# Distances between the addresses of streamed tiles and weights, one for each feed-forward stage of a decoder trunk, and the last stage streamed from its last column to its first

## The chip, the cores and the metric

The kernel runs on one core of a Trainium2 chip. The metric is the device time of one execution in microseconds (us). Before the change it is 1928.77 us, the median of two runs (1928.66 and 1928.88).

## The reference

Two decoder layers on 512 tokens of width 1024 in float32. Each layer is a feed-forward half-step, an attention and another feed-forward half-step; the first layer's attention is stick-breaking, the second's a sliding window with sinks.

```python
def swiglu(h, w_gate_up, w_down):
    gate, up = jnp.split(h @ w_gate_up, 2, axis=-1)
    return (jax.nn.silu(gate) * up) @ w_down
...
    for i in range(DEPTH):
        x = x + 0.5 * swiglu(rms_norm(x, norm_gains[i, 0]), ffn_w_gate_up[i, 0], ffn_w_down[i, 0])
        h = rms_norm(x, norm_gains[i, 1])
        ...
        x = x + 0.5 * swiglu(rms_norm(x, norm_gains[i, 2]), ffn_w_gate_up[i, 1], ffn_w_down[i, 1])
```

The inner width is 2816. The change concerns the four feed-forward stages, called 0 to 3 here; the stages run in the order 0, stick-breaking attention, 1, 2, sliding-window attention, 3.

## The kernel before

All activations are kept transposed: features on the 128 partitions, the 512 tokens as columns. A product of the width-1024 input is a sum over 8 blocks of 128 features, and every float32 operand is split into a high and a low float32r part, so that each term takes three matmuls: high weights by high input, high weights by low input, low weights by high input (`terms`). In each matmul a 128x128 block of weights is loaded into the array and a tile of 512 columns is streamed past it; the sum goes to a PSUM bank.

In a feed-forward stage (`ffn`), gate and up take 2 x 22 output tiles of 24 matmuls each, 1056 in all. Streamed are `xh0` to `xh7` and `xl0` to `xl7` (128 x 512 float32, 2048 bytes a partition), the weights lie in `whi` and `wlo`. The results leave PSUM through the vector engine and the scalar engine (`swiglu`), which write `hh0` to `hh21` and `hl0` to `hl21`. The down product has 8 output tiles of 66 matmuls, 528 in all; it streams the `hh` and `hl` tiles. The profile calls the two kinds of matmul `gu` and `dn` by their PSUM tiles.

Weights come as a stream of units (`queue`), each of 1024 or 896 columns, through rings of three buffers: a DMA writes `raw`, the scalar engine casts it to `whi` (L181), the vector engine (or GpSimd in the attentions) subtracts to get `wlo` (L186, L184). When the matmuls of a unit are done (`release`), the next unit is opened, cast and its successor's DMA issued. TensorE runs strictly in program order; all its matmuls are recorded by one helper and have line L75 in the profile, so they are told apart by their tiles. While one matmul streams its columns, the weights of the next are loaded.

The attentions' projections use the same ring. The input projections stream `xh` and `xl` (or stream weights past them), the output projections (PSUM tile `op`) stream the attention's `oh` and `ol`. At the start of the output projection of the sliding-window attention, weights are also put in spare tiles called `qw`.

Where tiles lie matters for this change. A pool places tiles one behind the other along the partition, in the order of their first use: constants, then the weight rings and the `xh`/`xl` tiles (pool `work`), then the pool of the stage. A block of weights is 512 bytes a partition, a streamed tile 2048, so within one stage all blocks of one weight tile, and all streamed tiles, have the same address modulo 128. In the program before, in bytes modulo 128: `whi` and `wlo` 96, `xh`/`xl` 96, `hh`/`hl` 64, the stick-breaking `oh`/`ol` 64, the window's `oh`/`ol` 96, `qw` 0. The distance, streamed address minus weight address, is then 0 in gate/up, 96 in down, 96 in the stick-breaking output projection, 0 in the window's, and 96 in the latter where the weights are in `qw`. (Modulo 512 the window's is 256, the others as said.)

Of the kernel before, what the change touches and what calls it, by code (L numbers as in the profile page):

```python
# [7 lines left out]
F32 = mybir.dt.float32  # L8
F32R = mybir.dt.float32r
# [6 lines left out]
P = 128  # L16
T = 512
TB = T // P
D = 1024
KD = D // P  # L20
# [4 lines left out]
HD = 64  # L25
PAIRS = HEADS // 2
CHUNKS = HEADS // 4
EPS = 1e-6
UNITS = 3
WARM = 40  # L30
POOL_SQUARES = 6
# [7 lines left out]
NROT = ROT // 2  # L39
# 500000 ** (-arange(0, 16, 2) / 16) in float32  # L40
INV_FREQ = [
# [23 lines left out]
class _Ordered:  # L65
    """an engine whose instructions stay in the order of the program"""

# [19 lines left out]
class _Filler:  # L87
    """tensor-engine work that fills the waits of an attention step: a generator that yields its cost,
    or None when nothing is ready"""

# [17 lines left out]
class _Trunk:  # L108
    def __init__(self, tc, pools, psum, aps):
        self.tc, self.nc = tc, _Engines(tc)  # L110
        self.const, self.work = pools
        self.psum = psum
        self.aps = aps
        self.units = []
        self.raw, self.ready = [], []
        self.taken = self.spent = 0
        self.roped = False
        self.extra = -1

# [1 line left out]
    def mm(self, out, lhs, rhs, start, stop):  # L121
        self.nc.tensor.matmul(out, lhs, rhs, start=start, stop=stop)

# [3 lines left out]
    def terms(self, out, pairs, first=True, last=True, release=()):  # L127
        """out = sum of w * x over pairs ((w_hi, w_lo), (x_hi, x_lo)): three float32r passes each;
        release: the terms that are the last of a unit of the weight stream, or 1: the last"""
        n = len(pairs)  # L130
        cost = 3 * max(out.shape[-1], 256) / 2400.0
        for i, ((wh, wl), (xh, xl)) in enumerate(pairs):
            self.mm(out, wh, xh, start=(first and i == 0), stop=False)
            self.mm(out, wh, xl, start=False, stop=False)
            self.mm(out, wl, xh, start=False, stop=(last and i == n - 1))
            if i in ((n - 1,) if release == 1 else release):
                self.release(1)
            yield cost
# [7 lines left out]

# [1 line left out]
    def queue(self, ap, pool=False):  # L148
        self.units.append((ap, ap.shape[1], pool))

    def _load(self, pieces=1):
# [8 lines left out]
    def _open(self, n):  # L160
        size = self.units[n][1]
        hi = self.work.tile([P, size], F32R, tag="whi", name=f"whi{n}", bufs=UNITS)
        lo = self.work.tile([P, size], F32R, tag="wlo", name=f"wlo{n}", bufs=UNITS)
        self.ready.append((hi, lo))

    def advance(self, hi, lo):
        """one more unit of the weight stream ahead, in tiles that the stage has free"""
        n = self.extra = len(self.ready)
        self.ready.append((hi, lo))
        self._part(n)  # L170
        self._load()
# [25 lines left out]
    def weights(self, a):  # L197
        """the next unit of the stream as [row, a, column] high and low parts"""
        hi, lo = self.ready[self.taken]
        self.taken += 1  # L200
        h3, l3 = (t.rearrange("p (a b) -> p a b", a=a) for t in (hi, lo))
        return [(h3[:, i, :], l3[:, i, :]) for i in range(a)]

# [1 line left out]
    def setup(self, which):  # L205
# [36 lines left out]

# [1 line left out]
    def norm_tile(self, k, which):  # L244
# [56 lines left out]

# [1 line left out]
    def swiglu(self, fp, f, gu):  # L303
# [12 lines left out]

    def ffn(self, following, first=False, rope=False):
        tc, nc = self.tc, self.nc
        with tc.tile_pool(name="ffn", bufs=1) as fp:
            hs, evac = [], []  # L320
            xs = list(zip(self.xh, self.xl))
            ahead = []
            if first:
                ahead = [(self.bank("gu"), self.weights(KD)) for _ in range(3)]
# [9 lines left out]
            for f in range(NF):  # L334
                gu = []
# [32 lines left out]

# [1 line left out]
    def stack(self, out, src):  # L370
        """a pair of heads (rows) to one [high | low] or [low | high] column of rows per head"""
        nc = self.nc
        for h in range(2):
            own, other = slice(h * HD, (h + 1) * HD), slice(HD - h * HD, 2 * HD - h * HD)
            nc.scalar.copy(out[own, h, :], src[own, :])
            nc.vector.tensor_sub(out[other, h, :], src[own, :], out[own, h, :])  # L376

    def project_pair(self, p, out, start=False):
        """q^T and k^T of a pair of heads, as exact high and low parts"""
        nc, ap = self.nc, self.ap  # L380
# [30 lines left out]
    def token_columns(self, evacuate, rows=None):  # L411
        """a chunk of 256 columns of an input projection, tokens on partitions"""
        w = self.weights(KD // 2) + self.weights(KD // 2)
        for b in range(TB):
            sl = slice(b * P, (b + 1) * P)
            ps = self.bank("tok")[:, : 4 * HD]
            yield from self.terms(ps, [((h[:, sl], l[:, sl]), w[k]) for k, (h, l) in enumerate(zip(self.xh, self.xl))], release=(KD // 2 - 1, KD - 1) if b == TB - 1 else ())
            if rows and b == 0:
                rows()
            evacuate(b, ps)  # L420

    def project_values(self, out):
        """v of four heads: [token, block, head, high | low]"""
        nc = self.nc
# [11 lines left out]
    def stick_scores(self, i, qk, out):  # L436
        """exclusive products of the kept lengths times beta, for one pair of heads and query block i"""
        nc, ap = self.nc, self.ap
# [25 lines left out]
    def stick_turn(self, i, beta, wt):  # L464
        """weights of query block i to keys on partitions, high and low parts"""
        nc = self.nc
# [47 lines left out]
    def fold(self, o, h, ps):  # L514
        """the products with the high and the low part of v are on rows of their own: add them"""
        t = self.ap.tile([HD, T], F32, tag="tmp", name="fold", bufs=2)
        self.nc.scalar.copy(t, ps[HD:, :])
        self.nc.vector.tensor_add(o[h * HD : (h + 1) * HD, :], ps[:HD, :], t)
# [8 lines left out]
    def project_early(self, parts, opened):  # L527
        """the first terms of the first output tiles, as far as parts are there"""
        self.settled, self.spare = len(parts), None
# [79 lines left out]

# [1 line left out]
    def rope_tables(self):  # L611
        """cos | cos and -sin | sin of every token's angles: [token, block, 16]"""
        self.roped = True
# [58 lines left out]

# [1 line left out]
    def rope(self, x, heads, engine):  # L674
        """x: [token, block, heads * HD], rotated in place"""
        nc, ap = self.nc, self.ap
# [11 lines left out]
    def head_factor(self, sq, heads, extra):  # L688
        """r * rsqrt(mean of squares of r * raw + eps) * extra, one per token, block, head"""
        nc, ap = self.nc, self.ap  # L690
# [57 lines left out]
    def window_queries(self, c, out):  # L748
        """four heads of q with head dims on partitions (two heads a tile), and their score factors"""
        nc, ap = self.nc, self.ap  # L750
# [20 lines left out]
    def window_scores(self, c, b, qt, y, out):  # L771
        """the softmax of four heads and one block of queries"""
        nc, ap = self.nc, self.ap
# [161 lines left out]

# [1 line left out]
    def store(self, n):  # L937
# [3 lines left out]
def build(tc, aps, stages="0s12w3"):  # L941
    from contextlib import ExitStack

    with ExitStack() as ctx:
# [4 lines left out]
        for st in stages:  # L949
            if st in "0123":  # L950
                i = int(st)
                for u in range(2 * NF):
                    net.queue(aps["gu"][i, u])
                for n in range(KD):
                    at = 0
                    for size in DOWN:
                        net.queue(aps["dn"][i, n, :, at * P : (at + size) * P])
                        at += size
# [18 lines left out]
        for i, st in enumerate(stages):  # L977
# [4 lines left out]
            if i == 0 and st in "0123":  # L982
                net.ffn(following, first=True)
                continue
            if stages[i + 1 : i + 2] == "w":
                net.ffn(following, rope=True)
                continue
            {"0": net.ffn, "1": net.ffn, "2": net.ffn, "3": net.ffn, "s": net.stick_breaking, "w": net.sliding_window}[st](following)

# [40 lines left out]
```

## Time and profile before

| what | value |
|---|---|
| median of two runs | 1928.77 us |
| span of the profiled execution | 1925.5 us |
| matmuls in it | 8994 |
| mean granted TensorE clock | 0.992 |
| gate/up of stages 0, 1, 2, 3 begins at | 32.7, 638.9, 1003.0, 1557.5 us |
| down of stages 0, 1, 2, 3 begins at | 250.3, 879.7, 1243.8, 1798.3 us |

The span runs from the first to the last instruction of the program; the time of a run has a few microseconds more around it. In the profile PE is TensorE's matmuls and PEld its weight loads, DVE the vector engine, ACT the scalar engine, POOL GpSimd, SP the engine that issues DMAs. [...] The chain of work that ended last is followed back from the last instruction, and its long pieces (start, duration, what, how many) give the time that so many matmuls took in a row.

### The profile page before, as it was taken

The page shows a single profiled execution, that of the slowest core. Times are in us where ns is not written, and L with a number is a line of the kernel's source. Part 1 is how long each engine was busy: PE and PEld are TensorE (multiplying, and loading weights), DVE is VectorE, ACT ScalarE, POOL GpSimd, SP SyncE. Part 2 cuts the span into 40 slices and gives each one's busy share as a digit, 9 for nine tenths or more (in the row PEclk, how much of TensorE's full clock was granted, in tenths as well). Part 3 has the DMA queues.
Part 4 walks back from the last instruction along what each step waited for, and adds up shares of the span by engine and source line. Part 5 has one row for each costly group of instructions (what it writes and reads, how often), then busy time and mean ns, then how long its engine had stood idle before and what let it go on. Part 6 is the DMA issues. An engine that isn't in the chain of part 4 may idle for free.

```text
span 1925.5 us, 22581 instructions
## 1 busy us (share of the span) xinstructions
PE 1895.7 (98%) x8994; PEld 1565.6 (81%) x8994; DVE 970.5 (50%) x1535; ACT 695.1 (36%) x1071; POOL 172.0 (9%) x131
## 2 busy tenths in 40 slices
PE   9999999999999999999999999999998999999999
PEld 7888888877887888888888888888887788888887
DVE  6444433378887644443235444423588664444321
ACT  5333222266675323332223333222357542223211
POOL 1000000233321000000000000000142210000000
PEclk9999999999999999999999999999989999999999
DMA  5233333321112333223333222333221122332331
GB/s 167 98 97 99 96 91 92 103 69 56 49 62 66 99 97 97 92 97 94 97 96 99 92 98 96 93 93 100 81 67 34 29 92 98 99 99 90 103 109 60
DMA packets 49930, 170.52 MB, mean 89 GB/s; under 512 B 5921, under 2 KB 6177, under 8 KB 49825
## 3 DMA queue, kind: packets, MB, share of 16 engines
q1 hardware_dynamic: 49824, 169.07, 27.9%
q8 instruction: 71, 1.16, 0.2%
q14 instruction: 35, 0.28, 0.0%
HBM read 166.96 MB, written 2.10 MB: 88 GB/s over the span
## 4 chain that ended last, share of the span: by engine, by line
PE 84%; DVE 8%; issue 4%; ACT 3%; POOL 1%; DMA 0%; SPq 0%; ACTq 0%; DVEq 0%; POOLq 0%
PE gu L75 49%; PE dn L75 23%; PE op L75 4%; PE tok L75 3%; DVE keep L459 2%; DVE beta L460 1%; PE pv L75 1%; DVE qs L376 1%; DVE wt L482 1%; ACT keep L453 1%; PE sc L75 1%; PE z L75 0%; PE ptr L75 0%; DVE e L793 0%; PE q L75 0%
## 5 line engine op out<-in xcount | busy, mean ns | idle before, releaser
L181 ACT CAST whi<-raw 128x1024 fp32r<-128x1024 f32 (+2 forms) x323 | 330.0, 1022 | 964.8 <-issue 361.6
L75 PE MATMUL gu<-xh,whi 128*128 128x512 f32 x1400 | 545.5, 390 | 1.4 <-ACT whi L181 1.4
L75 PE MATMUL gu<-xh,wlo 128*128 128x512 f32 x1400 | 545.0, 389 | 0.7 <-DVE wlo L186 0.7
L75 PE MATMUL gu<-xl,whi 128*128 128x512 f32 x1400 | 544.8, 389 | 0.5 <-DVE xl L253 0.5
L186 DVE TENSOR_TENSOR wlo<-raw,whi 128x1024 fp32r<-128x1024 f32 (+2 forms) x293 | 349.4, 1193 | 248.2 <-ACT whi L181 245.6
L75 PEld LDWEIGHTS gu<-xh,wlo 128*128 128x128 f32 x1400 | 262.8, 188 | 56.5 <-DVE wlo L186 1.8
L75 PEld LDWEIGHTS gu<-xh,whi 128*128 128x128 f32 x1400 | 262.9, 188 | 56.2 <-ACT whi L181 1.9
L75 PEld LDWEIGHTS gu<-xl,whi 128*128 128x128 f32 x1400 | 262.9, 188 | 55.3 <-DVE xl L253 0.9
L75 PE MATMUL dn<-hh,wlo 128*128 128x512 f32 x704 | 280.9, 399 | 0.0
L75 PE MATMUL dn<-hl,whi 128*128 128x512 f32 x704 | 277.4, 394 | 0.0
L75 PE MATMUL dn<-hh,whi 128*128 128x512 f32 x704 | 276.0, 392 | 0.0
L309 DVE TENSOR_TENSOR u<-gu,rbc 128x512 f32<-128x512 f32 x87 | 60.1, 691 | 274.7 <-PE gu L75 274.7
L75 PEld LDWEIGHTS dn<-hl,whi 128*128 128x128 f32 x704 | 132.1, 188 | 34.3
L75 PEld LDWEIGHTS dn<-hh,whi 128*128 128x128 f32 x704 | 132.2, 188 | 31.5
L75 PEld LDWEIGHTS dn<-hh,wlo 128*128 128x128 f32 x704 | 132.2, 188 | 30.5
L307 DVE TENSOR_TENSOR g<-gu,rbc 128x512 f32<-128x512 f32 x88 | 60.8, 691 | 176.5 <-PE gu L75 176.4
L261 POOL TENSOR_TENSOR acc<-acc,sq 128x512 f32<-128x512 f32 x30 | 46.4, 1547 | 1116.1 <-ACT sq L260 1116.1
L184 POOL TENSOR_TENSOR wlo<-raw,whi 128x512 fp32r<-128x512 f32 x60 | 87.5, 1483 | 164.9 <-ACT whi L181 164.9
L75 PE MATMUL tok<-whi,xh 128*128 128x256 f32 x288 | 86.4, 300 | 0.0
L75 PE MATMUL tok<-whi,xl 128*128 128x256 f32 x288 | 82.4, 286 | 0.1
L75 PE MATMUL tok<-wlo,xh 128*128 128x256 f32 x288 | 82.3, 286 | 0.1
L300 DVE SCALAR_TENSOR_TENSOR x<-dn,x 128x512 f32<-128x512 f32 x32 | 22.1, 691 | 116.5 <-PE dn L75 116.5
(310 smaller groups left out, 1957.4 us busy)
## 6 DMA issues: line engine op xcount, KB each, us to landing
raw<-in_gu_dram SPq DMA_DIRECT2D x173, 512.0 KB, 3.4
raw<-in_dn_dram SPq DMA_DIRECT2D x64, 448.0 KB, 3.3
raw<-in_dn_dram SPq DMA_DIRECT2D x32, 512.0 KB, 3.5
raw<-in_sbqk_dram SPq DMA_DIRECT2D x16, 512.0 KB, 3.4
raw<-in_swin_dram SPq DMA_DIRECT2D x10, 512.0 KB, 3.5
raw<-in_sbv_dram SPq DMA_DIRECT2D x8, 512.0 KB, 3.3
raw<-in_sbo_dram SPq DMA_DIRECT2D x8, 512.0 KB, 3.5
raw<-in_swo_dram SPq DMA_DIRECT2D x8, 512.0 KB, 3.3
```

The lines of the kernel that those rows point to most:

```text
L75: return self._tc.keep_in_program_order(method(*args, **kwargs))
L181: nc.scalar.copy(hi[:, s], raw[:, s])
L184: nc.gpsimd.tensor_sub(lo[:, t], raw[:, t], hi[:, t])
L186: nc.vector.tensor_sub(lo[:, s], raw[:, s], hi[:, s])
L261: (nc.gpsimd if k < POOL_SQUARES else nc.vector).tensor_add(self.acc, self.acc, sq)
L300: self.nc.vector.scalar_tensor_tensor(self.x[n], ps, factor, self.x[n], ALU.mult, ALU.add)
L307: nc.vector.tensor_mul(g, gu[0], self.rbc)
L309: nc.vector.tensor_mul(u, gu[1], self.rbc)
L376: nc.vector.tensor_sub(out[other, h, :], src[own, :], out[own, h, :])
L453: nc.scalar.activation(keep[:, :, :n], z[:, :, :n], AF.Sigmoid, scale=-0.125)
L459: nc.vector.tensor_tensor_scan(rev, rev, rev, 1.0, ALU.mult, ALU.bypass)
L460: nc.vector.tensor_mul(beta[:, :, : n - 1], beta[:, :, : n - 1], keep[:, :, 1:n])
```

## The change

Four things are edited.

- Weight tiles get 32 columns (128 bytes) of room each, and a unit's columns begin at a column of the stage's own: `WEIGHTS_AT`, 0, 8, 16 and 0 columns (0, 32, 64 and 0 bytes) for stages 0 to 3. The attentions' units begin at 0.
- Each feed-forward pool begins with a tile that nothing uses, of `GAPS` bytes: 416, 576, 736 and 416.
- In stage 3 (`BACKWARDS`), each matmul whose streamed operand is a plain tile of 512 columns gets both this operand and its PSUM output with a step of -1, from the last column to the first. The same sums land at the same places.
- `ffn` is told its stage. Comments are dropped, so later lines have other numbers.

```diff
+ROOM = 32
+
+WEIGHTS_AT = (0, 8, 16, 0)
+GAPS = (416, 416 + 160, 416 + 320, 416)
+BACKWARDS = (3,)
...
+    def shift(self, pool, size):
+
+        if size:
+            self.gaps += 1
+            pool.tile([P, size // 4], F32, name=f"gap{self.gaps}")
+
     def mm(self, out, lhs, rhs, start, stop):
+        if self.backwards and rhs.shape[-1] == T and len(rhs.shape) == 2:
+            out, rhs = out[:, ::-1], rhs[:, ::-1]
         self.nc.tensor.matmul(out, lhs, rhs, start=start, stop=stop)
...
-        hi = self.work.tile([P, size], F32R, tag="whi", name=f"whi{n}", bufs=UNITS)
-        lo = self.work.tile([P, size], F32R, tag="wlo", name=f"wlo{n}", bufs=UNITS)
-        self.ready.append((hi, lo))
+        at = self.form[n][0]
+        hi = self.work.tile([P, KD * P + ROOM], F32R, tag="whi", name=f"whi{n}", bufs=UNITS)
+        lo = self.work.tile([P, KD * P + ROOM], F32R, tag="wlo", name=f"wlo{n}", bufs=UNITS)
+        self.ready.append((hi[:, at : at + size], lo[:, at : at + size]))
...
         hi, lo = self.ready[self.taken]
+        backwards = self.form[self.taken][1]
         self.taken += 1
         h3, l3 = (t.rearrange("p (a b) -> p a b", a=a) for t in (hi, lo))
+        self.backwards = backwards
...
-    def ffn(self, following, first=False, rope=False):
+    def ffn(self, stage, following, first=False, rope=False):
         tc, nc = self.tc, self.nc
         with tc.tile_pool(name="ffn", bufs=1) as fp:
             hs, evac = [], []
+            self.shift(fp, GAPS[stage])
...
+                form = {"at": WEIGHTS_AT[i], "backwards": i in BACKWARDS}
                 for u in range(2 * NF):
-                    net.queue(aps["gu"][i, u])
+                    net.queue(aps["gu"][i, u], **form)
```

With the tiles as the built programs place them, the distance (streamed tile's first address minus weight address, modulo 128 bytes) becomes:

| stage | gate/up before | gate/up after | down before | down after |
|---|---|---|---|---|
| 0 | 0 | 0 | 96 | 0 |
| 1 | 0 | 96 | 96 | 0 |
| 2 | 0 | 64 | 96 | 0 |
| 3 | 0 | 0, columns backwards | 96 | 0, columns backwards |

Because each weight buffer is now 128 bytes longer than before, the three buffers of `whi` and of `wlo` no longer have the same address modulo 512; their distances modulo 512 are those of the table plus 0, 128, 256 or 384. Every engine's instructions stand in the order of before.

More of the change, by code (lines that the diff above doesn't have):

```diff
@@ L113, in __init__ @@
         self.aps = aps
-        self.units = []
+        self.units, self.form = [], []
         self.raw, self.ready = [], []
@@ L118, in __init__ @@
         self.extra = -1
+        self.gaps, self.backwards = 0, False
+    def shift(self, pool, size):
+        if size:
+            self.gaps += 1
+            pool.tile([P, size // 4], F32, name=f"gap{self.gaps}")
     def mm(self, out, lhs, rhs, start, stop):
+        if self.backwards and rhs.shape[-1] == T and len(rhs.shape) == 2:
+            out, rhs = out[:, ::-1], rhs[:, ::-1]
         self.nc.tensor.matmul(out, lhs, rhs, start=start, stop=stop)
@@ L145, in bank, with queue @@
         return self.psum.tile([P, T], F32, tag="mm", name=name, bufs=3)
-    def queue(self, ap, pool=False):
+    def queue(self, ap, pool=False, at=0, backwards=False):
         self.units.append((ap, ap.shape[1], pool))
+        self.form.append((at, backwards))
     def _load(self, pieces=1):
@@ L956, in build @@
                     for size in DOWN:
-                        net.queue(aps["dn"][i, n, :, at * P : (at + size) * P])
+                        net.queue(aps["dn"][i, n, :, at * P : (at + size) * P], **form)
                         at += size
@@ L982, in build @@
             if i == 0 and st in "0123":
-                net.ffn(following, first=True)
+                net.ffn(i, following, first=True)
                 continue
             if stages[i + 1 : i + 2] == "w":
-                net.ffn(following, rope=True)
+                net.ffn(int(st), following, rope=True)
                 continue
-            {"0": net.ffn, "1": net.ffn, "2": net.ffn, "3": net.ffn, "s": net.stick_breaking, "w": net.sliding_window}[st](following)
+            if st in "0123":
+                net.ffn(int(st), following)
+            else:
+                {"s": net.stick_breaking, "w": net.sliding_window}[st](following)
 def layout(x, positions, norm_gains, ffn_w_gate_up, ffn_w_down, sb_w_in, sb_w_out,
```

## The prediction

> **What bounds the kernel now.** I read the page's busy line and slices first, then the chain that ended last with its longest pieces, then the waits, and only then single instructions.
>
> ```profile
> span 1925.5 us, 22581 instructions
> PE 1895.7 (98%) x8994; PEld 1565.6 (81%) x8994; DVE 970.5 (50%) x1535; ACT 695.1 (36%) x1071; POOL 172.0 (9%) x131
> PEclk9999999999999999999999999999989999999999
> PE 84%; DVE 8%; issue 4%; ACT 3%; POOL 1%; DMA 0%; SPq 0%; ACTq 0%; DVEq 0%; POOLq 0%
> PE gu L75 49%; PE dn L75 23%; PE op L75 4%; PE tok L75 3%; DVE keep L459 2%; DVE beta L460 1%; PE pv L75 1%; DVE qs L376 1%; DVE wt L482 1%; ACT keep L453 1%; PE sc L75 1%; PE z L75 0%; PE ptr L75 0%; DVE e L793 0%; PE q L75 0%
> ```
>
> TensorE is busy 98% of the span at nearly full clock, and the gate/up products (`gu`) and down products (`dn`) of the four feed-forward stages are 72% of the chain. The waits say who waits for whom there.
>
> ```profile
> ACT whi L181 <- PE gu L75: 295.5, 99, 3.9
> ACT whi L181 <- PE dn L75: 277.6, 72, 4.7
> 1030.00:1230.00 200.00, 200.00 (x884) 165.65 (x883) 92.61 (x110) 60.25 (x74) 0.00 (x0) 1.00 0.30 97
> ```
>
> ScalarE waits for the matmuls to release weight buffers, not the other way round. In a 200 us stretch of gate/up (the columns are PE, PEld, DVE, ACT, POOL, clock, DMA share and GB/s) PE has no gap, DVE works 92.61 us and ACT 60.25 us. So in these stages the end is set by one number, the start-to-start time of a 512-column matmul, and whatever the change does to it falls on the time in full. The durations of the groups (390 ns) are pipelined and do not give it; a piece of the chain divided by its count does. These are the long pieces of the chain in order of time: start, us, what.
>
> ```profile
> 250.48 123.21 PE dn L75 x528
> 651.40 228.50 PE gu L75 x1008
> 879.91 123.21 PE dn L75 x528
> 1015.45 228.48 PE gu L75 x1008
> 1569.96 228.48 PE gu L75 x1008
> 1798.44 123.23 PE dn L75 x528
> ```
>
> Gate/up runs at 228.50 / 1008 = 226.7 ns a matmul, down at 123.21 / 528 = 233.4 ns, in every stage alike. The shapes are the same. The next fence has the matmuls (PE) and the weight loads (PEld) of a piece of down.
>
> ```profile
> 300.27 0.39 PE L75 MATMUL dn<-hl,whi 128*128 128x512 f32 x1
> 300.50 0.40 PE L75 MATMUL dn<-hh,wlo 128*128 128x512 f32 x1
> 300.27 0.19 PEld L75 LDWEIGHTS dn<-hh,wlo 128*128 128x128 f32 x1
> 300.50 0.19 PEld L75 LDWEIGHTS dn<-hh,whi 128*128 128x128 f32 x1
> ```
>
> The load of the next weights starts with the matmul before it, so one tile is streamed while another is read. In the kernel before, the distance between the two addresses is 0 modulo 128 bytes in gate/up and 96 in down. That alone could be a coincidence of stages. The output projections of the two attentions settle it: first a piece each of the chain, then a stretch of the timeline.
>
> ```profile
> 616.38 22.17 PE op L75 x95
> 1536.34 21.33 PE op L75 x94
> ```
>
> ```profile
> 1532.72 0.39 PE L75 MATMUL op<-oh,wlo 128*128 128x512 f32 x1
> 1532.95 0.39 PE L75 MATMUL op<-oh,whi 128*128 128x512 f32 x1
> 1533.17 0.39 PE L75 MATMUL op<-ol,whi 128*128 128x512 f32 x1
> 1533.40 0.39 PE L75 MATMUL op<-oh,wlo 128*128 128x512 f32 x1
> 1533.63 0.39 PE L75 MATMUL op<-oh,whi 128*128 128x512 f32 x1
> 1533.85 0.39 PE L75 MATMUL op<-ol,whi 128*128 128x512 f32 x1
> 1534.08 0.40 PE L75 MATMUL op<-oh,wlo 128*128 128x512 f32 x1
> 1534.32 0.39 PE L75 MATMUL op<-oh,qw 128*128 128x512 f32 x1
> 1534.55 0.40 PE L75 MATMUL op<-ol,qw 128*128 128x512 f32 x1
> 1534.79 0.62 PE L75 MATMUL op<-oh,qw 128*128 128x512 f32 x2
> 1535.25 0.40 PE L75 MATMUL op<-ol,qw 128*128 128x512 f32 x1
> 1535.48 0.39 PE L75 MATMUL op<-oh,qw 128*128 128x512 f32 x1
> 1535.71 0.40 PE L75 MATMUL op<-oh,whi 128*128 128x512 f32 x1
> ```
>
> In stick-breaking attention (distance 96) a matmul takes 22.17 / 95 = 233.4 ns, in sliding-window attention (distance 0) 21.33 / 94 = 226.9. And in the timeline the pace changes while tiles of one kind, `oh` and `ol`, are streamed: from 1532.72 to 1534.08 six matmuls with weights in `whi`/`wlo` (0) start 226.7 ns apart; from 1534.32 to 1535.71 six with weights in the spare tile `qw` (distance 96) start 231.7 ns apart. The two paces go with the distance, not with the stage or the place of the streamed tile.
>
> **The change part by part.** No engine gets, loses or reorders an instruction. Two matmuls of the last stage wait for one more semaphore, of TensorE itself, whose earlier work is in order anyway: 0. Adding 128 bytes to each weight tile and a gap tile costs memory alone. What changes is the pace of 4 x 1056 gate/up and 4 x 528 down matmuls, 226.7 and 233.4 ns now, a difference of 6.66 ns.
>
> A. Down in stages 0, 1 and 2 goes from distance 96 to 0 modulo 128: 3 x 528 x -6.66 ns = -10.6 us. Bounds: 0 if the stage keeps its pace, -10.6. I take -10.6. The tiles now lie at 0, 128, 256 and 384 modulo 512, and the trace has the quick pace at 0 (gate/up) and 256 (the window's projection) only; that is a rival below.
>
> B. Gate/up in stage 0 stays at 0 modulo 128: 0 us. The attentions stay too: the remainders modulo 128 of their matmuls are the same in both programs.
>
> C. Gate/up in stage 1 goes to 96, the distance at which down and both projections took 233.4: 1056 x 6.66 = +7.0 us. Bounds 0 and +7.0; I take +7.0.
>
> D. Gate/up in stage 2 goes to 64, which no row shows. Bounds: 0 at the pace of distance 0, +7.0 at that of 96. It is as far from one as half the period and nearer to the other, but the slow pace may be a narrow collision; I take the middle, +3.5 us.
>
> E. The last stage streams its 1584 matmuls backwards, from the last column to the first, and writes PSUM backwards. No row shows a negative step. Low end: everything at 226.7, 528 x -6.66 = -3.5 us. High end: the nearest row of a matmul that takes a column every second cycle, which is the one at half clock.
>
> ```profile
> 478.61 0.63 PE L75 MATMUL q<-xh,whi 128*128 128x512 f32 x1
> 479.46 0.63 PE L75 MATMUL q<-xh,wlo 128*128 128x512 f32 x1
> 477.30:480.60 3.30, 3.30 (x9) 2.62 (x10) 2.13 (x4) 3.07 (x4) 0.00 (x0) 0.50 0.02 5
> 1529.86 27.81 PE op L75 x120
> ```
>
> With the clock at 0.50 two matmuls take 0.85 us, 427 ns each, so half rate would cost 1056 x 200.3 + 528 x 193.6 = +314 us. Between the ends I go by the last row: the whole window projection, in which distances change under way, runs at 27.81 / 120 = 231.8 ns. When one stream goes down and the other up, the distance sweeps through all values, so a mixed pace is the nearest: 1056 x 5.1 - 528 x 1.6 = +4.5 us.
>
> A column is still four bytes next to the last one, and the half-rate end needs the memory to lose that. [...]
>
> Sum: -10.6 + 0 + 7.0 + 3.5 + 4.5 = +4.4 us, a span of 1929.9. The profiled execution's span of 1925.5 lies 3.3 us under the median of the two runs, 1928.77; the same 3.3 us around it make 1933.2 us, 0.2% above before. Nothing has to hide these terms, since TensorE itself changes pace; DVE and ACT would only wait a little more or less.
>
> **The rivals.** A measurement of this kernel can tell about 2%, 38.6 us, from no change.
>
> 1. Slower: descending columns break the one-column-per-cycle stream or the PSUM write. The place is the last stage alone. A to D add up to -0.1 us, so it decides the sign beyond 2% once E reaches 38.7 us, which is 253 ns a matmul over 1584 (39 us over the stage's present 362.6); at half rate the time is 1928.8 - 0.1 + 314 = 2243 us. For: nothing in the trace has a negative step. [...]
>
> 2. The distance does nothing, and the pace belongs to the tiles: down and backward streams stay as they are, 1928.8 us, or 1925.3 if only down of stage 0, whose streamed tiles now start at the same remainder as gate/up's, gains its 3.5 us. Against it stands the `qw` stretch. [...]
>
> 3. The period is 256 bytes or more, so 128 and 384 are not like 0. High and low parts of a weight lie an odd number of 128-byte steps apart now, and the distance changes within each triple. Everything forward then runs at the mixed pace: three gate/up stages 3 x 1056 x 5.1 = +16.2, three down stages -2.5, the last stage +4.5, some 768 attention matmuls +3.9; together +22.1, 1950.9 us. For: only 0 and 256 were seen to be quick.
>
> 4. Some distance, or the reversal, frees the pair altogether. The half-clock row says 512 columns need 427 / 2 = 213.5 ns, so gate/up carries 13.2 ns and down 19.9 ns of something. If stage 2 is freed, D is -13.9 and the time 1915.8; if the last stage is, E is -24.4 and the time 1904.3; if both, 1886.9. Against: the three pieces of gate/up shown above hold 3024 matmuls at 226.7. [...]
>
> **How the numbers follow.** The forecast (pace by distance modulo 128, backwards in between) gets 0.50, rival 1 0.13, rival 2 0.12, rival 3 0.16, rival 4 0.09. The predicted time is the forecast's, 1933.2 us. Its own range, with D and E at their small ends or at +7.0, is 1921.7 to 1939.2. The range for 8 in 10 goes down to 1912, which takes in rival 4 with stage 2 alone, and up to 1966, rival 3 and a backward pace of up to some 252 ns; left out are rival 1 and the larger half of rival 4. Faster by over 2% needs both parts of rival 4, 0.03; slower by over 2% is rival 1, 0.13; 0.84 lies within.
>
> **What would show it.** In the chain of the changed kernel the three first down pieces should read 528 matmuls in 119.7 us; stage 0's gate/up 226.7 ns, stage 1's 1008 matmuls in 235.2 us, stage 2's between 228.5 and 235.2, and the last stage's two pieces near 233.6 and 122.4. Down still at 123.2 would make A and the rule of distance wrong; gate/up of stage 0 above 228 would point to rival 3; and if the last stage's gate/up exceeds 255 us, E and the forecast fail together.

## The result and the profile after

The changed kernel takes 1949.53 us (median of 1948.56 and 1950.49) against 1928.77 before: a ratio of 1.0109, 95% interval 1.008 to 1.0138. It is slower by 20.8 us, inside the 2% that was named, but clear of the scatter of the runs (the two of the changed kernel lie 1.9 us apart, the two before 0.2). Its profiled execution has a span of 1946.7 us, 21.2 more than before. First the page's opening lines:

```profile
span 1946.7 us, 22582 instructions
PE 1917.4 (98%) x8994; PEld 1565.6 (80%) x8994; DVE 971.4 (50%) x1535; ACT 693.7 (36%) x1071; POOL 172.5 (9%) x131
```

The same matmuls, the same share of the span, and 21.7 us more of TensorE's time; the other engines are as before. The long pieces of the chain of work that ended last (start, us, what, how many; matmuls have line L80 now) say which stages took it:

```profile
33.87 222.74 PE gu L80 x960
256.61 122.56 PE dn L80 x528
656.57 235.20 PE gu L80 x1008
891.76 122.90 PE dn L80 x528
1027.17 234.26 PE gu L80 x1008
1261.43 78.61 PE dn L80 x339
1584.49 235.20 PE gu L80 x1008
1819.69 123.21 PE dn L80 x528
```

Two pieces of the kernel before are needed beside them, gate/up of stage 0 and the part of stage 2's down that lies on the chain:

```profile
32.88 217.60 PE gu L75 x960
1243.93 79.03 PE dn L75 x339
```

Every piece of gate/up is slower, stage 0's too (222.74 / 960 = 232.0 ns a matmul, before 217.60 / 960 = 226.7), whose distance modulo 128 didn't change. Stage 1 takes 233.3 ns, stage 2 232.4, stage 3 233.3. Down, which was to fall to 226.7 ns in stages 0 to 2, fell to 232.1, 232.8 and 231.9, and stayed at 233.4 in stage 3. The matmuls of stage 0 no longer start evenly (timeline, with starts printed in steps of 10 ns):

```profile
150.65 0.39 PE L80 MATMUL gu<-xh,whi 128*128 128x512 f32 x1
150.88 0.40 PE L80 MATMUL gu<-xl,whi 128*128 128x512 f32 x1
151.11 0.40 PE L80 MATMUL gu<-xh,wlo 128*128 128x512 f32 x1
151.35 0.39 PE L80 MATMUL gu<-xh,whi 128*128 128x512 f32 x1
151.57 0.40 PE L80 MATMUL gu<-xl,whi 128*128 128x512 f32 x1
```

Before, every start of gate/up came 226 or 227 ns after the last, which would print as 220 or 230; now there is a 240 among four gaps. Which matmuls lose is taken up with the first scan below.

Taken piece by piece and with the two pieces of 24 matmuls at the head of stages 1 to 3, gate/up lost 5.1, 6.9, 6.0 and 7.0 us and down gained 0.65, 0.3, 0.65 (78.61 against 79.03 for 339 of the 528 matmuls, taken for all) and 0.0: +23.3 us in all. The two attentions took 3.1 us less and the start-up 1.0 us more, which makes the 21.2 of the span.

### The profile page after: what moved, and what is told of

Its sections match the earlier page's. It is cut to its first block, busy times and chain, and to the rows that moved or that the text cites. A ratio compares the mean times of both kernels' runs of the same rounds, so it can differ in the third digit from the quotient of the medians.

```text
span 1946.7 us, 22582 instructions
## 1 busy us (share of the span) xinstructions
PE 1917.4 (98%) x8994; PEld 1565.6 (80%) x8994; DVE 971.4 (50%) x1535; ACT 693.7 (36%) x1071; POOL 172.5 (9%) x131
## 4 chain that ended last, share of the span: by engine, by line
PE 85%; DVE 7%; issue 4%; ACT 2%; POOL 1%; DMA 0%; SPq 0%; DVEq 0%; ACTq 0%; POOLq 0%
PE gu L80 50%; PE dn L80 23%; PE op L80 4%; PE tok L80 3%; DVE keep L478 2%; PE pv L80 1%; DVE beta L479 1%; PE q L80 1%; PE k L80 1%; DVE qs L395 1%; DVE wt L501 1%; PE z L80 1%; PE sc L80 1%; ACT keep L472 1%; PE ptr L80 0%
## 5 line engine op out<-in xcount | busy, mean ns | idle before, releaser
L80 PE MATMUL gu<-xh,wlo 128*128 128x512 f32 x1400 | 555.5, 397 | 0.2 <-DVE wlo L202 0.2
L80 PE MATMUL gu<-xh,whi 128*128 128x512 f32 x1400 | 553.7, 396 | 1.8 <-ACT whi L197 1.8
L80 PE MATMUL gu<-xl,whi 128*128 128x512 f32 x1400 | 554.2, 396 | 0.3 <-DVE xl L271 0.3
L80 PEld LDWEIGHTS gu<-xh,whi 128*128 128x128 f32 x1400 | 264.3, 189 | 64.3 <-ACT whi L197 2.3
L80 PEld LDWEIGHTS gu<-xl,whi 128*128 128x128 f32 x1400 | 263.3, 188 | 63.9 <-DVE xl L271 0.7
L80 PEld LDWEIGHTS gu<-xh,wlo 128*128 128x128 f32 x1400 | 263.2, 188 | 63.4 <-DVE wlo L202 1.8
L80 PE MATMUL dn<-hh,wlo 128*128 128x512 f32 x704 | 279.7, 397 | 0.0
L80 PE MATMUL dn<-hl,whi 128*128 128x512 f32 x704 | 278.9, 396 | 0.0
L80 PE MATMUL dn<-hh,whi 128*128 128x512 f32 x704 | 276.6, 393 | 0.0
L80 PEld LDWEIGHTS dn<-hh,whi 128*128 128x128 f32 x704 | 133.5, 190 | 31.4
L80 PEld LDWEIGHTS dn<-hl,whi 128*128 128x128 f32 x704 | 132.2, 188 | 31.8
L80 PEld LDWEIGHTS dn<-hh,wlo 128*128 128x128 f32 x704 | 132.2, 188 | 30.1
L80 PE MATMUL tok<-whi,xh 128*128 128x256 f32 x288 | 85.5, 297 | 0.0
L80 PE MATMUL tok<-wlo,xh 128*128 128x256 f32 x288 | 81.5, 283 | 0.1
L80 PE MATMUL tok<-whi,xl 128*128 128x256 f32 x288 | 81.4, 283 | 0.2 <-DVE xl L271 0.2
```

The lines of the kernel that those rows point to most:

```text
L80: return self._tc.keep_in_program_order(method(*args, **kwargs))
```

## The experiments

Theory 1: what counts is the distance modulo 256, so 128 isn't like 0; the room of 128 bytes, which makes high and low parts and neighbouring buffers differ by odd multiples of 128, is what costs. Its rival, theory 2: 128 is the period as predicted, and the loss comes from the backward streaming or from the tiles' new places. The first four runs go by these. Each ratio below is to runs of the kernel before from the same session, whose medians lay between 1923.8 and 1928.9 us.

**The room alone.** The kernel before with nothing but the room, written as settings of the changed kernel (`ROOM` stays 32):

```diff
-WEIGHTS_AT = (0, 8, 16, 0)
-GAPS = (416, 416 + 160, 416 + 320, 416)
-BACKWARDS = (3,)
+WEIGHTS_AT = (0, 0, 0, 0)
+GAPS = (0, 0, 0, 0)
+BACKWARDS = ()
```

> The kernel before with nothing but the 128 bytes of room in each weight tile (no gap tiles, columns forward, units at column 0). Theory 1, the pace goes by the distance modulo 256 and a distance that changes within each triple of matmuls keeps it slow: gate/up goes from 226.7 to the 232 ns that stage 0 of the changed kernel shows, in all four stages, 4 x 1056 x 5.3 = +22 us, down stays at 233 to 234 (its distances become 96 and 224 modulo 256), the attentions' projections lose 1 to 4 us: 1951 to 1955 us. Theory 2, only the distance modulo 128 counts and the loss of the change is made elsewhere (backwards streaming, the tiles' new places): 1928.8 us, gate/up at 226.7.

Measured: 1951.2 us, ratio 1.012 (1.0098 to 1.0141). Pieces of gate/up in stages 0 and 1:

```profile
35.22 222.74 PE gu L80 x960
659.54 233.87 PE gu L80 x1008
```

232.0 ns each. So memory that no instruction touches costs as much as the whole change, with all columns forward and the distances modulo 128 as before. So the loss needs no backward streaming, and distances that are the same modulo 128 gave another pace. The room also moves the tiles behind it, which theory 2 names too; that is left to the runs on places below (e8_pad).

**The last stage forward.** The changed kernel with:

```diff
-BACKWARDS = (3,)
+BACKWARDS = ()
```

> The changed kernel with the last stage streamed forward. Theory 1 (the mixed distances set the pace, reversal only adds a little): the last stage reads as stage 0 does, 232.0 ns in gate/up and 232.1 in down in place of 233.3, 1584 x -1.3 = -2 us, 1947.5 us. Theory 2 (the reversal is what costs): the last stage falls to 226.7 ns, 1584 x -6.6 = -10.5 us, 1939 us.

Measured: 1949.77 us, ratio 1.0118 (1.0101 to 1.0135). The last stage's pieces:

```profile
1588.54 233.89 PE gu L80 x1008
1822.43 122.57 PE dn L80 x528
```

232.0 and 232.1 ns, as in stage 0, so theory 1's pace came; the 1.3 and 0.6 us that these pieces gained are too small to see between medians whose runs lie 2 us apart. In the changed kernel the reversal isn't where the time went.

**Down at distance 0, nothing else.** The kernel before with a gap tile in each feed-forward pool, written as settings of the changed kernel:

```diff
-ROOM = 32
-WEIGHTS_AT = (0, 8, 16, 0)
-GAPS = (416, 416 + 160, 416 + 320, 416)
-BACKWARDS = (3,)
+ROOM = 0
+WEIGHTS_AT = (0, 0, 0, 0)
+GAPS = (416, 416, 416, 416)
+BACKWARDS = ()
```

> The kernel before with nothing but a gap tile of 416 bytes in each feed-forward pool, so that down too has distance 0 modulo 512. Theories 1 and 2 alike: down falls from 233.4 to 226.7 ns, 4 x 528 x -6.66 = -14.1 us, 1914.7 us, faster than both kernels. If the distance does nothing: 1928.8 us, down at 233.4.

Measured: 1914.79 us, ratio 0.9933 (0.9912 to 0.9953), faster than both kernels.

```profile
252.36 119.68 PE dn L80 x528
878.00 119.68 PE dn L80 x528
649.48 228.52 PE gu L80 x1008
```

Down runs at 119.68 / 528 = 226.7 ns, gate/up stays. That the distance sets the pace was right; that 128 is its period was not.

**Backwards at distance 0.** As the last, with `BACKWARDS = (3,)`.

> As e3_align, with the last stage streamed backwards at distance 0. If backwards streaming has a pace of its own, whatever the distance: the last stage at the 233.3 ns of the changed kernel, 1584 x 6.6 = +10.5 us over e3_align, 1925.2 us. If its 233.3 ns came from the mixed distances: as e3_align, 1914.7 us, the last stage at 226.7.

Measured: 1924.78 us, ratio 0.9988 (0.9977 to 0.9998).

```profile
1559.18 235.20 PE gu L80 x1008
1794.38 123.22 PE dn L80 x528
```

233.3 and 233.4 ns: backward streaming has a pace of its own, and here, where forward would have 226.7, it costs 10.0 us.

**The scan of distances.** The question was now whether 128 is slow by itself or only in a mixture, and whether any distance is better than 0. Gap tiles set the distance of down, a different one in each stage and constant over it; gate/up stays at 0.

```diff
-GAPS = (416, 416, 416, 416)
+GAPS = (448, 480, 32, 64)
```

> A scan: the kernel before with gap tiles that set the distance of down to 32, 64, 128 and 160 bytes in stages 0 to 3, constant over the stage; gate/up stays at 0. If 128 is slow by itself (period 256): stage 2's down at 233 to 234 ns. If 128 is as quick as 0 and only a distance that changes from matmul to matmul costs (period 128): 226.7. For 32, 64 and 160 theory 1 gives 226.7 to 234 (0 and 96 being the known points); a rival by which some distance frees the pair altogether would show 213 to 224 ns in one of them. Time between 1915 and 1929 us by theory 1.

Measured: 1926.27 us, ratio 0.9981 (0.9967 to 0.9995). Down at 32, 64, 128 and 160:

```profile
250.30 123.20 PE dn L80 x528
880.44 120.87 PE dn L80 x528
1242.22 79.01 PE dn L80 x339
1797.29 123.71 PE dn L80 x528
```

233.3, 228.9, 233.1 and 234.3 ns. So 128 is slow by itself.

That is not the whole loss of a mixture, though. In stage 0 of the changed kernel the built program puts the weights of 536 of the piece's 960 gate/up matmuls at distance 0 and of 424 at 128 (modulo 256). The mean of the two constant paces, 226.7 and 233.1, would be 229.5 ns; 232.0 was measured. Sorting 954 gaps of that trace shows why: a gap from one start to the next is 226.9 ns on average where both the weights in use and those loaded meanwhile lie at 0 (227 gaps), and 233.2 to 234.3 where one or both lie at 128 (727 gaps). In this sorting one block at 128 slows two gaps. The kernel with the room alone gives 226.9 and 233.2 to 234.2 ns in stage 1. In stage 2, with 64 and 192, the same sorting gives 229.3 to 235.4 ns without such an order.

```diff
-GAPS = (448, 480, 32, 64)
+GAPS = (96, 128, 160, 224)
```

> The scan goes on: down at 192, 224, 256 and 320 bytes in stages 0 to 3. Period 256: 256 reads 226.7 as 0 does, and 320 reads what 64 read in the scan's first half. A period of 512 or more: 256 still 226.7 (the window's projection showed it), but 320 differs from 64. 224 should be like neighbours of 96 or better, 226.7 to 234 ns. Time between 1915 and 1929 us.

Measured: 1922.28 us, ratio 0.9968 (0.9954 to 0.9981). Down at 192, 224, 256 and 320:

```profile
251.59 123.20 PE dn L80 x528
882.12 123.20 PE dn L80 x528
1246.11 76.82 PE dn L80 x339
1795.90 120.89 PE dn L80 x528
```

233.3, 233.3, 226.6 and 229.0 ns: 256 reads as 0, 320 as 64. The period is 256 bytes as far as two pairs can tell.

**Gate/up at 64.** A 64-byte pad between the weight rings and the input tiles moves gate/up in all four stages; `GAPS` of 352 sets down to 0.

```diff
         if k == 0:
             self.xh, self.xl = [], []
+            if len(self.raw) < 2 * UNITS:
+                w.tile([P, 16], F32, name="between")
```

> A pad of 64 bytes between the weight rings and the input tiles, so that gate/up has the constant distance 64 in all stages; down is set to 0. Theory 1: down 226.7 (-14.1 us), gate/up at the pace that the scan gives for 64, between 226.7 and 234, so 1915 to 1946 us, and the same for gate/up as for down at 64, since only the distance counts. If the pace belongs to the stage's tiles: gate/up differs from down at 64 by more than 2 ns.

Measured: 1918.52 us, ratio 0.9944 (0.9921 to 0.9967).

```profile
650.60 230.73 PE gu L80 x1008
881.34 119.73 PE dn L80 x528
```

230.73 / 1008 = 228.9 ns, what down took at 64: the pace goes with the distance, whichever tiles have it. The time is lower than 1914.8 plus the pieces' loss of about 9 us, and the trace has the rest in the sliding-window attention, not in the feed-forward stages. These are that attention's stretches, of the kernel with down at distance 0 and then of this one (after the stretch: us, busy times, clock, DMA share, GB/s):

```profile
1357.70:1549.30 191.60, 178.12 (x1130) 156.96 (x1130) 140.99 (x426) 106.28 (x266) 59.25 (x49) 0.94 0.16 52
```

```profile
1363.50:1549.50 186.00, 170.07 (x1131) 148.37 (x1130) 140.91 (x426) 105.89 (x266) 59.36 (x49) 0.97 0.17 54
```

5.6 us shorter at a granted clock of 0.97 in place of 0.94. Such a difference lies between executions: the kernel with down at distance 0 had one run of 1909.72 us at a mean clock of 0.995, and this kernel's run at 0.995 took 1918.09, 8.4 us more and near the 9 of the pieces. It is why the pieces, and not the medians, decide about single nanoseconds here. Whether the pad, which moves that attention's tiles as well, has a part in it was not tried.

**All addresses moved by 32 bytes.** As the kernel with down at distance 0, with a pad ahead of everything:

```diff
+        c.tile([P, 8], F32, name="pad")
         warm = c.tile([P, P], BF16, name="warm")
```

> As e3_align, with 32 unused bytes ahead of all tiles, so that every address moves by 32 and every distance stays. If only distances count: 1914.8 us, gate/up and down at 226.7. If a tile's own place modulo 64, 128 or 256 counts: another pace, up to 233 ns in gate/up and down, up to 1957 us.

Measured: 1915.2 us, ratio 0.9939 (0.992 to 0.9958).

```profile
650.70 228.52 PE gu L80 x1008
879.23 119.68 PE dn L80 x528
```

Both paces stay at 226.7 ns. A tile's own place doesn't count, as far as 32 bytes tell; the distance does.

**Reading and writing backwards apart.** As the kernel backwards at distance 0, but `mm` reverses one side only; gate/up's results then stand in reversed order, and down's output puts them right.

```diff
-            out, rhs = out[:, ::-1], rhs[:, ::-1]
+            if self.reading:
+                rhs = rhs[:, ::-1]
+            else:
+                out = out[:, ::-1]
...
+            self.reading = False
             for n in range(KD):
                 ps = self.bank("dn")
```

> As e4_backwards (distance 0), but in the last stage gate/up only reads its columns backwards and writes PSUM forward, so that the inner values stand in reversed order, and down reads them forward and writes PSUM backwards, which puts them right again. If the 6.7 ns of reversal come from reading: gate/up 233.3, down 226.7, 1914.8 + 7.0 = 1921.8 us. If from writing PSUM: gate/up 226.7, down 233.3, 1918.3 us. If each alone costs it: 1925.2 us.

Measured: 1922.5 us, ratio 0.9967 (0.9951 to 0.9982).

```profile
1560.61 235.20 PE gu L80 x1008
1795.81 119.71 PE dn L80 x528
```

Reading backwards costs all of it, 233.3 ns; writing PSUM backwards costs nothing, 226.7.

**A finer scan.** As the kernel with down at distance 0, with the inner tiles 256 bytes longer and their data begun at column 4, 12, 20 and 60 in stages 0 to 3.

```diff
+FINE = (4, 12, 20, 60)
...
-        hi = fp.tile([P, T], F32R, name=f"hh{f}")
-        lo = fp.tile([P, T], F32R, name=f"hl{f}")
+        hi = fp.tile([P, T + 64], F32R, name=f"hh{f}")[:, self.fine : self.fine + T]
+        lo = fp.tile([P, T + 64], F32R, name=f"hl{f}")[:, self.fine : self.fine + T]
...
             self.shift(fp, GAPS[stage])
+            self.fine = FINE[stage]
```

> A finer scan: as e3_align with 256 more bytes in each inner tile and its columns begun at 4, 12, 20 and 60 columns in stages 0 to 3, so that down has the distances 16, 48, 80 and 240 modulo 256, constant over the stage. If the quick distances are isolated, at 0 and in part at 64: 233 to 234 ns in all four, 1914.8 + 14 = 1929 us. If there is a zone round 0 or round 64: 227 to 230 at 16 and 240, or at 48 and 80, about 1922 us. If a distance frees the pair altogether: below 226 ns.

Measured: 1925.77 us, ratio 0.9992 (0.9982 to 1.0003). Down at 16, 48, 80 and 240:

```profile
251.23 122.32 PE dn L81 x528
880.76 123.20 PE dn L81 x528
1244.76 78.28 PE dn L81 x339
1797.24 123.22 PE dn L81 x528
```

231.7, 233.3, 230.9 and 233.4 ns. None beats 0; just above 0 and 64 the pace lies between quick and slow (16 and 80), just below them it is fully slow (240 and 48). Neither picture that was on record, isolated points or a zone on both sides, is quite right.

**Stick-breaking's output projection too.** As the kernel with down at distance 0, with

```diff
         with tc.tile_pool(name="stick", bufs=1) as self.ap:
+            self.shift(self.ap, 160)
```

> As e3_align, with a gap tile of 160 bytes at the head of the stick-breaking pool as well, so that its output projection gets distance 0 modulo 256 too (155 more matmuls at 0). Theory 1: that projection falls from 233.4 to 226.7 ns, 155 x -6.66 = -1.0 us, 1913.8 us; the pool's other distances, between its own tiles, stay, those to the weights change for single matmuls only. If the distance doesn't count there: 1914.8 us.

Measured: 1911.2 us, ratio 0.9926 (0.9902 to 0.9949); its four runs go from 1910.36 to 1915.85, those of the kernel without the pad from 1909.72 to 1916.4. The projection's piece, without the pad and with it:

```profile
604.91 32.18 PE op L80 x138
```

```profile
603.54 31.36 PE op L80 x138
```

The 0.8 us that the piece gained is near the 1.0 expected; the medians are too close to tell the two apart. Both beat the kernel before and the changed one.

**Everything backwards.** `BACKWARDS = (0, 1, 2, 3)` without room; down at 32, 64, 160 and 224.

> All four feed-forward stages streamed backwards, gate/up at distance 0 and down at 32, 64, 160 and 224 in stages 0 to 3 (the first column read lies 4 bytes under that, modulo 256). If reading backwards costs the same at every distance: 233.3 ns everywhere, 4 x 1056 x 6.66 = +28 us, 1957 us. If backwards too has quick distances: one of the down pieces falls to 226.7 or 228.9 ns, 119.7 or 120.9 us in place of 123.2.

Measured: 1955.91 us, ratio 1.0158 (1.0114 to 1.0201). The four pieces of down, and gate/up of stage 1:

```profile
259.26 123.20 PE dn L80 x528
896.59 123.20 PE dn L80 x528
1267.56 79.02 PE dn L80 x339
1825.80 123.21 PE dn L80 x528
661.39 235.20 PE gu L80 x1008
```

233.1 to 233.4 ns at every distance tried, also in stage 1, whose first column read lies four bytes under 64, where forward takes 228.9. The 233.1 is the piece of 339, and down at 96 before reads the same there (79.03 / 339) against 233.4 in the whole pieces.

All constant forward distances together, ns a matmul (80 and 128 from pieces of 339):

| distance modulo 256 | 0 | 16 | 32 | 48 | 64 | 80 | 96 | 128 | 160 | 192 | 224 | 240 |
|---|---|---|---|---|---|---|---|---|---|---|---|---|
| ns | 226.7 | 231.7 | 233.3 | 233.3 | 228.9 | 230.9 | 233.4 | 233.1 | 234.3 | 233.3 | 233.3 | 233.4 |

## Why the prediction was right and wrong

The time lay in the stated range and within 2%, but the likeliest forecast, 1933.2 us with its own range of 1921.7 to 1939.2, was not what happened. Rival 3, with a chance of 0.16, came nearest, at 1950.9 us against 1949.5 measured.

- **What bounds the kernel** held. The change acted on the start-to-start time of 512-column matmuls and fell on the span in full: +23.3 us in these pieces, +21.2 in the span.
- **The distance sets the pace** held, and is now shown: with one gap tile in its pool down runs at 226.7 ns (e3_align), gate/up at 64 has the pace of down at 64 (e7_gu64), and moving all addresses alike changes nothing (e8_pad).
- **The step that failed is the period.** Terms A and B took 128, 256 and 384 for 0 because the trace showed only 0 and 256 to be quick. A was to bring -10.6 us and brought -1.6; B was to be 0 and cost 5.1. Constant 128 takes 233.1 ns (e5_scan_a), and the room alone costs as much as the whole change (e1_room_alone). The two terms make 14.1 of the 18.9 us between forecast and pieces. By the constant paces of 0 and 128 alone A would have been about -5.7 and B about +3.0, an estimate from the scans and the places in the built program; the other 6 us are the extra cost of a mixture, which the prediction didn't have either.
- **C**, +7.0, measured +6.9. It was right by luck of the place: modulo 256 stage 1 got both 96 and 224, and both are slow (233.4 and 233.3 ns where constant).
- **D**, +3.5 as a middle, measured +6.0. Constant 64 takes 228.9 ns, 2.2 over the best, so the middle was near for the distance that was meant; but two remainders, 64 and 192, took turns, and 192 takes 233.3. The mean of the constant paces would be 231.4, or +4.9 us; here too the mixture cost more.
- **E**, +4.5 by a mixed pace, measured +7.0. The picture behind it, two streams that sweep past each other, gave too small a size in both parts: gate/up lost 7.0 where 5.4 was put, and down, put at -0.8, gained nothing. Backward reading runs at the one steady pace of 233.1 to 233.4 ns that most distances have forward. The half rate of rival 1 didn't come: descending columns cost 6.6 ns a matmul on the reading side at distance 0, and writing PSUM backwards costs nothing (e9_read_write).
- **Rival 3's sum** was right through errors that cancel, with a mixed pace that fitted by chance (below): its attention term of +3.9 isn't there (the two output projections' pieces changed by -0.1 and +0.6 us, and the attentions as a whole got shorter), while stages 1 and 3 lost more than its mixed pace.

The mixed pace of 231.8 ns, which E and rival 3 use, was read from a piece that is hardly a mixture. In the built program six of its 120 matmuls have another distance than 0, and its first two are slow starts:

```profile
1529.86 0.49 PE L75 MATMUL op<-oh,whi 128*128 128x512 f32 x1 [0.46 <-ACT oh L839]
1530.32 0.50 PE L75 MATMUL op<-ol,whi 128*128 128x512 f32 x1
1530.66 0.40 PE L75 MATMUL op<-oh,wlo 128*128 128x512 f32 x1
```

These two gaps of 0.46 and 0.34 us are 0.35 us longer than two of 226.7 ns. Over 120 matmuls that is 2.9 ns of the 5.1 by which the piece's mean lies above 226.7. That a real mixture of 0 and 128 then took 232.0 ns is luck.

Rivals 2 and 4 are out: the distance does count, and in 12 forward distances and the backward ones no constant pace below 226.6 ns came up (76.82 / 339, down at 256).

What stays open: why 0 and 64 are good. A conflict between reading the streamed tile and loading the next weights would fit the constant distances. It doesn't say by itself why a block at 128 also slows the gap in which it is used, and no run removed the loads, so it is argued, not shown. The mixture of 64 and 192 is unexplained. Distances finer than 16 bytes were not tried.

## What to carry to other kernels

Where matmuls stand back to back, divide a long piece of the chain by its count, stage by stage; equal shapes with unequal paces (226.7 and 233.4 ns here) can come from where tiles lie, and an unused tile of 416 bytes in each of four stages was worth some 13 us (e3_align, ratio 0.9933). Before taking two equal remainders for the same case, look for the next larger period: a pad, a longer buffer or a ring whose stride is an odd multiple of half the period changes the distance from matmul to matmul (with the room the ring's stride is 33 x 128 bytes, and gate/up went from 226.7 to 232.0 ns, e1_room_alone). Let a probe keep each thing constant over a stage; this change mixed two remainders in every stage and could not show what any one of them does.

## What the runs showed of the hardware that was not expected

- The pace depends on the distance modulo 256 bytes, as far as two pairs can tell (226.7 ns at 0 and 226.6 at 256, 228.9 at 64 and 229.0 at 320; e3_align, e5_scan_a, e6_scan_b), with a best point at 0 (226.7 ns for 512 float32r columns), a second at 64 (228.9), and 233 to 234 ns at most others; 16 and 80 lie between (231.7 and 230.9, e10_fine).
- Where 0 and 128 take turns, a matmul keeps the quick pace (226.9 ns on average over 227 gaps of the changed kernel's stage 0) only if both its own weights and those loaded during it lie at 0; the other 727 gaps take 233.2 to 234.3 ns on average.
- A streamed operand read from its last column to its first takes 233.1 to 233.4 ns at every distance tried (e4_backwards, e12_back_scan). Descending columns in the PSUM output cost nothing (119.71 us for 528 matmuls in e9_read_write, against 119.68 forward in e3_align).
